# A hybrid DeltaNet and attention decoder in float32: the weights' low halves moved off GpSimd, intermediate results written into PSUM banks, and the output norm taken once per group of heads

## The chip, the cores and the metric

The kernel runs on one core of a Trainium2 chip. The metric is device time in microseconds (us) for one execution of the whole program. Engines are named as the profile names them: PE is TensorE (PEld its weight loads), DVE is VectorE, ACT is ScalarE, POOL is GpSimd and SP is SyncE, which here issues the DMAs. Each engine works through its own instructions in the order in which the program lists them, and an instruction starts when the semaphores that it waits for allow it.

## What is computed

A decoder trunk of two layers on 272 tokens (16 meta tokens and 256 of input) of width 2048, all in float32. Layer 0 mixes tokens by a gated DeltaNet, layer 1 by differential attention. Each has a squared-relu MLP of width 8192, and RMS norms stand around every part. Cut to what matters here, the DeltaNet is:

```python
proj = h @ w_in                                  # 2048 -> q, k, v, z, b, a
qkv  = silu(causal_depthwise_conv(qkv, conv_w))  # 4 taps
q, k = l2_normalize(q) * 128**-0.5, l2_normalize(k)
beta = sigmoid(b); g = -exp(a_log) * softplus(a + dt_bias)
o = chunk_gated_delta_rule(q, k, v, beta, g)     # a state S of 128 x 128 per head, by chunks
o = rms_norm(o, o_norm) * silu(z)                # the output norm, per head and token
mix = o @ w_out
h = h + rms_norm(mix, gain)
```

There are 16 query and key heads and 32 value heads of 128. The delta rule solves a unit triangular system per chunk and head, adds a correction to the state S, and reads S with the queries.

## The kernel before, in words

Activations lie with features on the 128 partitions and the 272 tokens along the row. Every float32 product is made of three fast ones (`mm3`, L147 to L159). A weight tile of 128x2048 arrives by DMA as `wraw`. `load_w` (L119 to L145) treats it in two halves of 1024 columns: ACT copies each to `whi`, a rounded type (L137), and another engine subtracts this from the raw half to give `wlo` (L141), here called the low half. PE then multiplies `whi` with `xh` (L154), `wlo` with `xh` (L157) and `whi` with `xl` (L158) for each of 16 blocks of 128. The second matmul of a half needs its low half. In the DeltaNet three `whi` and three `wlo` buffers rotate, each of half a tile; in the MLPs there are three more.

Which engine does L141 is decided at L138 to L140: while `ring["pool"]` is set, which is the whole DeltaNet, every second half of a tile goes to POOL and of the first halves every other one, and the rest goes to DVE. Outside the DeltaNet DVE does it, but for the first three tiles of three stages (two MLPs' and the query projection's), which POOL does while DVE is busy with a norm.

The DeltaNet (`gdn`) works on 8 groups of 4 value heads. PE's projections run without end: 12 tiles of `w_in` per group (4 for queries and keys, 4 for values, 4 for the gates z) and 4 tiles of `w_out` for the group two behind. The group's other work is written as Python generators in `Flow`, a list of tasks with due times. Each matmul of the projections advances a clock, and a task that is due places its instructions there; so the small matmuls of the delta rule stand among the projections, with the yields (`STEP`, `OTURN`, `SLACK` and so on) as distances. The build then sets the order within each engine. `tc.high_priority()` around a weight's halves puts them ahead.

The places that the prediction touches, in the order of a group:

- `conv_silu`, L606: four taps on a projection in PSUM (L615 on ACT, L618 on DVE), a tanh (L620, ACT, into the SBUF tile `cv_x`) and the product of both (L621, DVE, to `kq` or `vt`).
- `products`: norms of keys and queries, then for each chunk the products `ps_u`, multiplied by decays on DVE into `UA` (L711). POOL masks `UA` (L733, L826).
- `solve` with `forward`: 30 dependent small DVE instructions (L629, L630) on the 16x16 blocks.
- `core`: for each of three chunks of tokens (128, 128, 16) a chain of small matmuls through two PSUM banks (`bank`, tag "c") with an ACT or DVE instruction between each two. `w` is copied by ACT (L909), `ws` is `w` times a factor (L913, DVE), `ps_s2` the state's correction and `S` the new state (L925). `ps_o` is the output and `ov` its combination with the state's part (L936). Then the output norm: squares with sums on ACT (L942, into `o2`), eleven instructions of four columns on DVE (L944 to L948, with `rsqrt` at L105 to L111), and the scaling of `ov` by DVE (L949). `turned` transposes the result on PE (L809) and multiplies it by the gate (L811).
- `gate_out`: the product with `w_out`, added to `acc` by DVE (L982). For the last group each finished row block is also squared on ACT (`add_ss`, L183, or L185 on DVE for the last two) and summed into `ss` by DVE (L190), for the norm of the mix. `ss` goes to PE as `pst` (L213), and from there the first MLP begins.

Of the kernel before, what the change touches and what calls it, by code (L numbers as in the profile page):

```python
# [30 lines left out]
G1 = 8  # L31
GB = 4
HOLD = 1
QGAP = 3.0
# [1 line left out]
NSQ = 2  # L36
# [10 lines left out]
STEP7 = (2.0, 5.0, 35.0)  # L47
SLACK, UGAP, SOLVE, STEP, OTURN = 6.0, 1.2, 40.0, 3.0, 14.0
SQ = 2
PQ = 2  # L50
WARM = (2, 6, 8)
LAMBDA_INIT = 0.8 - 0.6 * math.exp(-0.3 * 1)
NEG = -1.0e30
# [34 lines left out]
def trunk(ctx: ExitStack, tc: tile.TileContext, a):  # L88
    nc = tc.nc
# [5 lines left out]
    npool = ctx.enter_context(tc.tile_pool(name="npool", bufs=2))  # L95
# [18 lines left out]
    ring = {"i": 0, "pools": [wpool] * 3, "spare": []}  # L114

    flow = Flow()
# [6 lines left out]
    def load_w(src, urgent=2, after=None):  # L123
        raw = load_raw(src)
        his, los = [], []
        with tc.high_priority() if urgent == 2 else ExitStack():
            for q in range(2):
                part = raw[:, q * HD:(q + 1) * HD]
                room = ring["spare"].pop(0) if ring["spare"] else None
                if room is None:  # L130
                    pool = ring["pools"][ring["i"] % len(ring["pools"])]
                    ring["i"] += 1
                    hi = pool.tile([P, HD], F32R, tag="whi", name="whi")
                    lo = pool.tile([P, HD], F32R, tag="wlo", name="wlo")
                else:
                    hi, lo = room
                nc.scalar.activation(hi, part, AF.Copy)  # L137
# [3 lines left out]
                inst = eng.tensor_tensor(lo, part, hi.bitcast(F32), ALU.subtract)  # L141
# [31 lines left out]
        pool, tag, bufs = ring["rows"]  # L173
        return pool.tile([P, L], F32, tag=tag, name=name, bufs=bufs)

    def add_ss(ss, src, m, N, eng):

        if m == 0:
            ss.append(npool.tile([P, L], F32, tag="ss", name="ss", bufs=1))
            return [nc.scalar.activation(ss[0][:, :N], src, AF.Square)]  # L180
        sq = npool.tile([P, L], F32, tag="sq", name="sq", bufs=SQ)
        if m < KT - NSQ or eng is nc.gpsimd:
            one = nc.scalar.activation(sq[:, :N], src, AF.Square)  # L183
# [6 lines left out]
        return [one, eng.tensor_tensor(ss[0][:, :N], ss[0][:, :N], sq[:, :N], ALU.add)]  # L190

    def squares(m, N, ss, acc, gi, after=None):

        inst = add_ss(ss, acc[:, m, :N], m, N, nc.vector)[-1].ins
# [87 lines left out]

    xh = xpool.tile([P, KT, L], F32R, tag="xh", name="xh")
    xl = xpool.tile([P, KT, L], F32R, tag="xl", name="xl")
    r0 = npool.tile([P, L], F32, name="r0", bufs=1)
    unscaled = {}
    with tc.tile_pool(name="ps0", bufs=2, space=bass.MemoryType.PSUM) as ps0:
        ring["p"] = v0
# [47 lines left out]
    ring["pool"] = True  # L336
# [4 lines left out]
    ring["pool"] = False  # L341


    qpool = ctx.enter_context(tc.tile_pool(name="qpool", bufs=1))
# [146 lines left out]
    ssm, e = mlp(0, L, xh, xl)  # L491
# [12 lines left out]
def gdn(ctx, tc, a, e):  # L504
    nc = tc.nc
    const, npool, dram, psm = (e[k] for k in ("const", "npool", "dram", "psm"))
# [3 lines left out]
    load_w, mm3, rsqrt, xh, xl, new_acc, ssm = (e[k] for k in ("load_w", "mm3", "rsqrt", "xh", "xl", "new_acc", "ssm"))  # L510
    squares, flow, r0 = e["squares"], e["flow"], e["r0"]
# [17 lines left out]
    def work(name):  # L529
        return gt.tile([P, HB, P], F32, tag="g1", name=name, bufs=G1)  # L530

# [75 lines left out]
    def conv_silu(ps, m, out):  # L607

        ac = gt.tile([P, L], F32, tag="g272", name="cv_a", bufs=GB)
        th = gt.tile([P, L], F32, tag="g272", name="cv_x", bufs=GB)  # L610
        x = ps
        if m in unscaled:
            x = th
# [6 lines left out]
        nc.scalar.activation(th, ac, AF.Tanh, scale=0.5)  # L620
        nc.vector.scalar_tensor_tensor(out, th, 1.0, ac, ALU.add, ALU.mult)  # L621

# [171 lines left out]
    def core(b, g):  # L794
# [7 lines left out]
        def turned(c, o, n, ov):  # L802

            while g["gates"] < HB:
                yield 1.0
            oT = g["oT"]
            pT = psc.tile([P, 512], F32, tag="c", name="ps_ot")
            for hv in range(HB):
                nc.tensor.transpose(pT[:, hv * n:(hv + 1) * n], ov[:n, hv], ident[:n, :n])  # L809
# [7 lines left out]
        step = STEP7[0] if b == NB - 1 else STEP  # L817
        merged = {}

        def flat(t):  # L820
# [38 lines left out]
        for c, (o, n) in enumerate(CH):  # L859
            if c == 0:  # L860
                R = nv[0]
            else:
# [12 lines left out]
                ov = work("ov")  # L875
# [29 lines left out]
                nc.tensor.matmul(pw[:n, hv], dt[:, hv, :], z[:n, hv], start=True, stop=True)  # L905
            if c == 2:
                g["free"] = True
            w = work("w")
            nc.scalar.copy(w[:n], pw[:n])  # L909
            if c < 2:  # L910
                ws = work("ws")
                sb = sup[:, c].rearrange("p h r -> p (h r)")[:, :, None].broadcast_to([P, HB, P])
                nc.vector.tensor_tensor(ws, w, sb, ALU.mult)  # L913
            yield step
            if c < 2:
                pS2, pS2v = bank("ps_s2")
# [19 lines left out]
                    nc.vector.scalar_tensor_tensor(ov[:n, hv], ov[:n, hv], eG[:n, c, HB * b + hv:HB * b + hv + 1],  # L936
                                                   po[:n, hv], ALU.mult, ALU.subtract)

            o2 = work("o2")
            ms = gt.tile([P, HB], F32, tag="o_ms", name="o_ms")  # L940
            for hv in range(HB):
                nc.scalar.activation(o2[:n, hv], ov[:n, hv], AF.Square, accum_out=ms[:n, hv:hv + 1])  # L942
            rqc = rq[:n, c].rearrange("p h r -> p (h r)")
            nc.vector.tensor_tensor(ms[:n], ms[:n], rqc, ALU.mult)  # L944
            nc.vector.tensor_tensor(ms[:n], ms[:n], rqc, ALU.mult)
            nc.vector.tensor_scalar(ms[:n], ms[:n], 1.0 / P, EPS, ALU.mult, ALU.add)
            ri = rsqrt(ms[:n], "rso", [P, HB], n)
            nc.vector.tensor_tensor(ri[:n], ri[:n], rqc, ALU.mult)  # L948
            nc.vector.tensor_tensor(ov[:n], ov[:n], ri[:n, :, None].broadcast_to([n, HB, P]), ALU.mult)  # L949
            g["chunk"] = c + 1  # L950
            flow.add(turned(c, o, n, ov), STEP7[1] if b == NB - 1 else OTURN)
            yield step

    def halves(g):
# [11 lines left out]
    def gate_out(b, g):  # L966

        if b == 0:
            flow.add(halves(g))
        flow.until(lambda: "halves" in g)  # L970
        oh, ol = g["halves"]
        for mq in range(4):
            hi, lo = load_w(a["w_out"][b, mq])
            for j in range(4):
                m = 4 * mq + j
                ps = psm.tile([P, 512], F32, tag="m", name="ps_out")
                mm3(ps[:, :L], hi, lo, 4 * j, oh, ol, HB, 0, L)
                with tc.high_priority():
                    if b == 0:
                        nc.scalar.copy(acc[:, m, :], ps[:, :L])  # L980
                    else:
                        added = nc.vector.tensor_tensor(acc[:, m, :], acc[:, m, :], ps[:, :L], ALU.add)  # L982
                    if b == NB - 1 and m > 0:
                        squares(m - 1, L, ssm, acc, 1, added)
                        if m == KT - 1:
                            squares(m, L, ssm, acc, 1)
        if b + 1 < NB:
            flow.add(halves(gs[b + 1]))

# [269 lines left out]
```

## Time and profile before

| what | value |
|---|---|
| median of 3 runs (lowest, highest) | 3111.37 us (3111.28, 3116.6) |
| the profiled execution, its own time | 3111.88 us |
| its span, first to last instruction | 3110.1 us |
| PE busy | 3010.9 us, 97% of the span |
| DVE busy | 1930.1 us, 62% |
| ACT busy | 1443.3 us, 46% |
| POOL busy | 660.7 us, 21% |
| mean granted TensorE clock | 0.987 of full |

The rows of the profile name a line, an engine, the operation, what is written and read (buffer numbers left out), the shape and the count. Then come the busy time, the mean of one in ns, and the idle time of that engine just before, with what ended it. A waits view sums such idle time by who waited for whom. A windows view gives for a stretch of time the busy time of each engine with its number of instructions, then the granted TensorE clock, the share of the DMA engines and GB/s. A timeline lists start, duration and instruction. A busy PE is not a PE at its peak, since matmuls overlap and their ends are modelled: the number of matmuls in a stretch says more than its busy time.

### The profile page before, as it was taken

The numbers are of one execution on the slowest core, as the hardware profiler recorded it, in microseconds if no ns is written. First come the engines' busy times: TensorE is split into PE (matmuls) and PEld (weight loads), VectorE is DVE, ScalarE is ACT, GpSimd is POOL, SyncE is SP. The second block draws the span as 40 slices with busy tenths as digits, with TensorE's granted clock in tenths as the row PEclk, the third lists the DMA queues.
The fourth block names the chain that finished last, engine by engine and source line by source line (L and its number), as shares of the span: only waits on it lengthen the run. The fifth ranks groups of instructions, "written<-read, shape, count | busy, mean of one in ns | idle before, by whom it ended". The sixth has DMA issues, their size and how long they took to land. (4 is left out here: it accounts for less than half of the span.)

```text
span 3110.1 us, 57337 instructions
## 1 busy us (share of the span) xinstructions
PE 3010.9 (97%) x23779; PEld 2946.4 (95%) x23779; DVE 1930.1 (62%) x3449; ACT 1443.3 (46%) x2565; POOL 660.7 (21%) x398
## 2 busy tenths in 40 slices
PE   7999999999998889999999999999999999999998
PEld 6988999999998889999999999999999999999998
DVE  7676574766748485455555557777756555555555
ACT  4445454454544345434444334555555444444443
POOL 2544445545454351000000003400004000000000
PEclk9999999999999989999999999999999999999999
DMA  4433334334343335454444443443354555555553
GB/s 178 151 117 122 133 118 151 133 125 158 117 152 103 119 145 183 176 176 172 171 174 175 176 176 123 177 149 136 138 189 163 189 186 183 188 189 180 188 190 109
DMA packets 92468, 488.36 MB, mean 157 GB/s; under 512 B 29104, under 2 KB 32528, under 8 KB 34736
## 3 DMA queue, kind: packets, MB, share of 16 engines
q1 hardware_dynamic: 92208, 484.70, 43.7%
q8 instruction: 187, 3.06, 0.4%
q14 instruction: 73, 0.60, 0.1%
HBM read 481.41 MB, written 3.25 MB: 156 GB/s over the span
## 5 line engine op out<-in xcount | busy, mean ns | idle before, releaser
L137 ACT ACTIVATE whi<-wraw 128x1024 fp32r<-128x1024 f32 x890 | 939.2, 1058 | 1180.3 <-PE ps_dn L158 435.9
L141 DVE TENSOR_TENSOR wlo<-wraw,whi 128x1024 fp32r<-128x1024 f32 x682 | 841.4, 1237 | 717.1 <-ACT whi L137 715.9
L141 POOL TENSOR_TENSOR wlo<-wraw,whi 128x1024 fp32r<-128x1024 f32 x208 | 503.7, 2424 | 1584.3 <-ACT whi L137 1572.5
L158 PE MATMUL ps_dn<-yl,whi 128*128 128x272 f32 (+1 forms) x2048 | 584.5, 285 | 0.0
L157 PE MATMUL ps_dn<-yh,wlo 128*128 128x272 f32 (+1 forms) x2048 | 583.2, 285 | 0.0
L154 PE MATMUL ps_dn<-yh,whi 128*128 128x272 f32 (+1 forms) x2048 | 583.2, 285 | 0.0
L154 PE MATMUL ps_up<-xh,whi 128*128 128x272 f32 (+1 forms) x2048 | 582.9, 285 | 0.0
L158 PE MATMUL ps_up<-xl,whi 128*128 128x272 f32 (+1 forms) x2048 | 582.0, 285 | 0.1
L157 PE MATMUL ps_up<-xh,wlo 128*128 128x272 f32 (+1 forms) x2048 | 581.5, 285 | 0.2 <-DVE wlo L141 0.2
L154 PE MATMUL ps_in<-xh,whi 128*128 128x272 f32 x1520 | 463.4, 305 | 0.0
L157 PE MATMUL ps_in<-xh,wlo 128*128 128x272 f32 x1520 | 442.4, 291 | 16.7 <-DVE wlo L141 13.3
L158 PE MATMUL ps_in<-xl,whi 128*128 128x272 f32 x1520 | 444.0, 292 | 3.3 <-DVE xl L319 3.3
L154 PEld LDWEIGHTS ps_up<-xh,whi 128*128 128x128 f32 x2048 | 386.2, 189 | 0.5 <-ACT xh L402 0.2
L158 PEld LDWEIGHTS ps_dn<-yl,whi 128*128 128x128 f32 x2048 | 386.6, 189 | 0.0
L154 PEld LDWEIGHTS ps_dn<-yh,whi 128*128 128x128 f32 x2048 | 386.3, 189 | 0.0
L158 PEld LDWEIGHTS ps_up<-xl,whi 128*128 128x128 f32 x2048 | 385.6, 189 | 0.3 <-DVE xl L410 0.3
L157 PEld LDWEIGHTS ps_dn<-yh,wlo 128*128 128x128 f32 x2048 | 385.2, 188 | 0.0
L157 PEld LDWEIGHTS ps_up<-xh,wlo 128*128 128x128 f32 x2048 | 384.7, 188 | 0.5 <-DVE wlo L141 0.5
L157 PEld LDWEIGHTS ps_in<-xh,wlo 128*128 128x128 f32 x1520 | 290.2, 191 | 20.3 <-DVE wlo L141 14.9
L154 PEld LDWEIGHTS ps_in<-xh,whi 128*128 128x128 f32 x1520 | 289.7, 191 | 7.8 <-issue 5.1
L158 PEld LDWEIGHTS ps_in<-xl,whi 128*128 128x128 f32 x1520 | 289.5, 190 | 4.8 <-DVE xl L319 3.7
L399 POOL TENSOR_TENSOR hT<-hT,t_res 128x272 f32<-128x272 f32 (+1 forms) x40 | 34.9, 894 | 742.9 <-DVE t_res L391 698.2
(305 smaller groups left out, 4833.8 us busy)
## 6 DMA issues: line engine op xcount, KB each, us to landing
wraw<-w_up SPq DMA_DIRECT2D x128, 1024.0 KB
wraw<-w_down SPq DMA_DIRECT2D x128, 1024.0 KB
wraw<-w_in SPq DMA_DIRECT2D x97, 1024.0 KB
wraw<-w_out SPq DMA_DIRECT2D x32, 1024.0 KB
wraw<-w_kv SPq DMA_DIRECT2D x32, 1024.0 KB
wraw<-w_q SPq DMA_DIRECT2D x16, 1024.0 KB
wraw<-w_o SPq DMA_DIRECT2D x16, 1024.0 KB
gb<-g_dram SPq DMA_DIRECT2D x8, 544.0 KB
```

The costliest lines, as they stand in the source:

```text
L137: nc.scalar.activation(hi, part, AF.Copy)
L141: inst = eng.tensor_tensor(lo, part, hi.bitcast(F32), ALU.subtract)
L154: one = nc.tensor.matmul(ps, wh, rh, start=(k == 0), stop=False)
L157: nc.tensor.matmul(ps, wl, rh, start=False, stop=False)
L158: ring["mm"] = nc.tensor.matmul(ps, wh, rl, start=False, stop=(k == nk - 1))
L399: put(key, eng.tensor_tensor(h, h, ts[m][:, :N], ALU.add))
```

## The change

All of it is in the DeltaNet, and in names and constants around it:

1. **Low halves.** The choice at L138 to L140 becomes `nc.gpsimd if not urgent else nc.vector`, and `ring["pool"]` goes. In the program POOL's L141 falls from 208 instructions to 18 (those first three tiles of three stages), and 190 move to DVE.
2. **Tanh through the bank.** `conv_silu` writes the tanh back into the projection's own PSUM bank, and L621 reads it there in place of `cv_x`.
3. **`ws` by ACT.** Four activations of 128x128 with a factor per partition read `ps_w` and write `ws`; only then comes the copy to `w`. The DVE instruction of 128x512 (L913) goes.
4. **The output norm per group.** The squares are written into the PSUM bank of `ps_o` in place of `o2`. In groups 0 to 6 the eleven small DVE instructions run once for the three chunks (12 columns) in place of three times (4 columns). Each chunk's `ov` is scaled by four activations on ACT in place of L949. The three transposes then follow at `OTURN`, `OTURN + 2` and `OTURN + 4`. In the last group the norm stays per chunk, with ACT's four activations.
5. **Squares of the mix through banks.** In the last group's `gate_out` a square is written by ACT into the PSUM bank of the row block that has just been added to `acc`, and `ss` adds it from there. The squares of the last two row blocks move from DVE to ACT too.
6. **Room.** `G1`, the number of 128x512 work tiles, goes from 8 to 9, and `r0` shares the buffer of `ss`.

```diff
-                ring["n"] = ring.get("n", 0) + 1
-                on_pool = ring.get("pool") and (q == 1 or ring["n"] // 2 % PQ == 1)
-                eng = nc.gpsimd if not urgent or on_pool else nc.vector
+                eng = nc.gpsimd if not urgent else nc.vector
...
-    def add_ss(ss, src, m, N, eng):
+    def add_ss(ss, src, m, N, eng, bank=None):
...
-        sq = npool.tile([P, L], F32, tag="sq", name="sq", bufs=SQ)
-        if m < KT - NSQ or eng is nc.gpsimd:
+        if bank is None or m == KT - 1:
+            sq = npool.tile([P, L], F32, tag="sq", name="sq", bufs=SQ)
+        else:
+            sq = bank
+        if m < KT - NSQ or eng is nc.gpsimd or bank is not None:
             one = nc.scalar.activation(sq[:, :N], src, AF.Square)
...
-        th = gt.tile([P, L], F32, tag="g272", name="cv_x", bufs=GB)
...
+        th = ps[:, :L]
         nc.scalar.activation(th, ac, AF.Tanh, scale=0.5)
         nc.vector.scalar_tensor_tensor(out, th, 1.0, ac, ALU.add, ALU.mult)
...
+            if c < 2:
+                ws = work("ws")
+                for hv in range(HB):
+                    nc.scalar.activation(ws[:, hv], pw[:, hv], AF.Copy, scale=sup[:, c, hv // 2, hv % 2:hv % 2 + 1])
             w = work("w")
             nc.scalar.copy(w[:n], pw[:n])
-            if c < 2:
-                ws = work("ws")
-                sb = sup[:, c].rearrange("p h r -> p (h r)")[:, :, None].broadcast_to([P, HB, P])
-                nc.vector.tensor_tensor(ws, w, sb, ALU.mult)
...
-            o2 = work("o2")
-            ms = gt.tile([P, HB], F32, tag="o_ms", name="o_ms")
             for hv in range(HB):
-                nc.scalar.activation(o2[:n, hv], ov[:n, hv], AF.Square, accum_out=ms[:n, hv:hv + 1])
...
-            nc.vector.tensor_tensor(ov[:n], ov[:n], ri[:n, :, None].broadcast_to([n, HB, P]), ALU.mult)
+                nc.scalar.activation(po[:n, hv], ov[:n, hv], AF.Square, accum_out=ms[:n, c, hv:hv + 1])
+            outs.append((c, o, n, ov))
+            if b == NB - 1 or c == len(CH) - 1:
...
+                ri = rsqrt(mc, "rso%d" % k, [P, k], pn)
+                nc.vector.tensor_tensor(ri, ri, rqc, ALU.mult)
+                for i, (cc, oo, nn, ot) in enumerate(outs):
+                    for hv in range(HB):
+                        nc.scalar.activation(ot[:nn, hv], ot[:nn, hv], AF.Copy, scale=ri[:nn, HB * i + hv:HB * i + hv + 1])
+                    flow.add(turned(cc, oo, nn, ot), STEP7[1] if b == NB - 1 else OTURN + TGAP * i)
```

Lines after the first edit move by up to ten: L139 of the changed kernel is L141 of the one before, L191 is L190, L616 is L618, L620 is L621, L710 is L711, L927 is L925, L938 is L936 and L991 is L982.

On DVE, in a group of the middle, where the second chunk's state `S` and output `ov` are formed, the kernel before has, with `oT` the gated output and `o_ms` the sums of squares:

```order
L811 SCALAR_TENSOR_TENSOR oT<-ps_ot,gain_h,oT 128x4x128
L621 SCALAR_TENSOR_TENSOR vt<-cv_x,cv_a 128x272
L711 SCALAR_TENSOR_TENSOR UA_4838<-ps_u,sc_nc,dec 16x32
L913 TENSOR_TENSOR ws<-w,sc_sup 128x512
L925 SCALAR_TENSOR_TENSOR S<-S,eGL,ps_s_4910 128x128 x4
L936 SCALAR_TENSOR_TENSOR ov<-ov,eG,ps_o 128x128 x4
L618 SCALAR_TENSOR_TENSOR cv_a<-ps_in,gdnc,cv_a 128x271
L618 SCALAR_TENSOR_TENSOR cv_a<-ps_in,gdnc,cv_a 128x270
L944 TENSOR_TENSOR o_ms<-o_ms,sc_rq 128x4
```

At the same place of the changed kernel's DVE there stands:

```order
L139 TENSOR_TENSOR wlo<-wraw,whi 128x1024
L620 SCALAR_TENSOR_TENSOR vt<-ps_in,cv_a 128x272
L710 SCALAR_TENSOR_TENSOR UA_4763<-ps_u,sc_nc,dec 16x32 x2
L927 SCALAR_TENSOR_TENSOR S<-S,eGL,ps_s_4832 128x128
L139 TENSOR_TENSOR wlo<-wraw,whi 128x1024
L927 SCALAR_TENSOR_TENSOR S<-S,eGL,ps_s_4832 128x128 x3
L938 SCALAR_TENSOR_TENSOR ov<-ov,eG,ps_o 128x128 x4
L616 SCALAR_TENSOR_TENSOR cv_a<-ps_in,gdnc,cv_a 128x271
```

`ws` and the norm's small instructions are gone from here, `vt` reads the tanh from the bank `ps_in`, and two low halves stand in the queue, one of them between the first and the other three parts of `S`.

On ACT, near a group's end, where the third chunk's squares are taken and the gates' tanh (`zt`) follow, the kernel before has:

```order
L942 ACTIVATE o_8289,o_ms<-ov 16x128 x4
L137 ACTIVATE whi<-wraw 128x1024
L790 ACTIVATE zt<-ps_in 128x272
L772 ACTIVATE nv<-ps_v,sc_nk 128x128 x2
L772 ACTIVATE nv<-ps_v,sc_nk 16x128
L137 ACTIVATE whi<-wraw 128x1024 x2
L790 ACTIVATE zt<-ps_in 128x272
```

There the changed kernel's ACT has, with the scaling of the three chunks' `ov` at L957:

```order
L137 ACTIVATE whi<-wraw 128x1024 x2
L789 ACTIVATE zt<-ps_in 128x272
L137 ACTIVATE whi<-wraw 128x1024
L957 ACTIVATE ov<-ov,rs_y 128x128 x8
L137 ACTIVATE whi<-wraw 128x1024
L957 ACTIVATE ov<-ov,rs_y 16x128 x4
L789 ACTIVATE zt<-ps_in 128x272
```

Eight activations that wait for DVE's `rs_y` now stand between two upper halves of weights, and four more behind.

More of the change, by code (lines that the diff above doesn't have):

```diff
@@ L30 @@
 LAG = 2
-G1 = 8
+G1 = 9
 GB = 4
@@ L49 @@
 SQ = 2
-PQ = 2
+TGAP = 2.0
 WARM = (2, 6, 8)
@@ L190, in add_ss, with squares @@
         return [one, eng.tensor_tensor(ss[0][:, :N], ss[0][:, :N], sq[:, :N], ALU.add)]
-    def squares(m, N, ss, acc, gi, after=None):
-        inst = add_ss(ss, acc[:, m, :N], m, N, nc.vector)[-1].ins
+    def squares(m, N, ss, acc, gi, after=None, bank=None):
+        inst = add_ss(ss, acc[:, m, :N], m, N, nc.vector, bank)[-1].ins
         if m < PRE[gi // 2]:
@@ L284, in trunk @@
     xl = xpool.tile([P, KT, L], F32R, tag="xl", name="xl")
-    r0 = npool.tile([P, L], F32, name="r0", bufs=1)
+    r0 = npool.tile([P, L], F32, tag="ss", name="r0", bufs=1)
     unscaled = {}
@@ L334, in trunk @@
     nc.vector.tensor_scalar(nlam, nlam, -1.0, None, ALU.mult)
-    ring["pool"] = True
     ssm = []
@@ L609, in conv_silu @@
         ac = gt.tile([P, L], F32, tag="g272", name="cv_a", bufs=GB)
-        th = gt.tile([P, L], F32, tag="g272", name="cv_x", bufs=GB)
         x = ps
         if m in unscaled:
-            x = th
+            x = gt.tile([P, L], F32, tag="g272", name="cv_x", bufs=GB)
             nc.vector.tensor_tensor(x, ps[:, :L], r0, ALU.mult)
@@ L817, in core @@
         step = STEP7[0] if b == NB - 1 else STEP
+        outs = []
+        ms = gt.tile([P, len(CH), HB], F32, tag="o_ms", name="o_ms")
+        nc.vector.memset(ms, 1.0)
         merged = {}
@@ L983, in gate_out @@
                     if b == NB - 1 and m > 0:
-                        squares(m - 1, L, ssm, acc, 1, added)
+                        squares(m - 1, L, ssm, acc, 1, added, spent)
                         if m == KT - 1:
-                            squares(m, L, ssm, acc, 1)
+                            squares(m, L, ssm, acc, 1, None, ps)
+                spent = ps
         if b + 1 < NB:
```

17 lines of the change are left out of this document (9 added, 8 removed).

## The prediction

> **What bounds the kernel now.** The first view read is the table of windows: PE's, PEld's, DVE's, ACT's and POOL's busy time with its count of instructions, then the granted clock, the DMA share and GB/s. Its rows are the DeltaNet without its start and end, the end of the DeltaNet, and a stretch of the MLP.
>
> ```profile
> 60.00:1088.00 1028.00, 973.24 (x7459) 932.45 (x7457) 663.61 (x1499) 490.67 (x1118) 491.95 (x258) 0.98 0.37 130
> 1088.00:1137.00 49.00, 37.21 (x247) 36.20 (x248) 36.09 (x50) 18.17 (x31) 26.30 (x12) 0.80 0.49 176
> 1400.00:1800.00 400.00, 400.00 (x3174) 400.00 (x3173) 216.59 (x265) 164.93 (x202) 0.00 (x0) 1.00 0.49 174
> ```
>
> In the MLP PE never stops: 3174 matmuls in 400 us, 0.126 us each, at full clock. Nothing there can be shortened by this change. In the DeltaNet's body PE stands still for 1028 − 973.2 = 54.8 us, and its clock averages 0.98, worth at most 0.02 × 1028, about 20 us. At the end another 11.8 us of 49 are idle. So about 85 us can be had at all, between 30 and 1137 us. The DMAs are busy 0.37 of the time and aren't the limit.
>
> Second comes the waits view of PE for 30 to 1135 us: who waited for whom, us in all, times, the longest.
>
> ```profile
> PE ps_in L157 <- DVE wlo L141: 12.8, 6, 5.2
> PE pst L213 <- DVE ss L190: 10.6, 1, 10.6
> PE ps_s L918 <- DVE ws L913: 9.8, 7, 3.4
> PE ps_ot L809 <- DVE ov L949: 8.1, 3, 4.5
> PE ps_u L705 <- DVE UA L711: 6.8, 5, 1.4
> PE ps_out L154 <- DVE acc L982: 4.8, 5, 2.5
> PE ps_g L579 <- issue: 3.5, 1, 3.5
> PE ps_in L157 <- POOL wlo L141: 3.4, 4, 1.6
> ```
>
> Nearly every row names DVE, which is busy only 663.6 of 1028 us, 65%. So the question is why a DVE with time to spare comes late. Third, then, are the timelines (start, duration, instruction) of DVE and of POOL around one such wait:
>
> ```profile
> 553.89 2.27 DVE L109 SCALAR_TENSOR_TENSOR rs_t<-rs_t 128x12 f32<-128x12 f32 x1
> ...
> 565.48 2.40 DVE L621 SCALAR_TENSOR_TENSOR vt<-cv_x,cv_a 128x272 f32<-128x272 f32 x1
> ```
>
> ```profile
> 553.77 2.36 POOL L141 TENSOR_TENSOR wlo<-wraw,whi 128x1024 fp32r<-128x1024 f32 x1 [2.37 <-ACT whi L137]
> 565.19 2.38 POOL L141 TENSOR_TENSOR wlo<-wraw,whi 128x1024 fp32r<-128x1024 f32 x1 [9.06 <-ACT whi L137]
> ```
>
> A DVE instruction on 12 columns takes 2.27 us and ends at 556.16; POOL's low half, which began just before it, ends at 556.13. The product `vt` ends at 567.88, POOL's next at 567.57. An instruction that meets POOL's low half stands until that is over. What decides which instructions do this shows in DVE's groups (busy us, mean ns | idle before) and in the tile view of `acc` (min/median/max ns):
>
> ```profile
> L141 DVE TENSOR_TENSOR wlo<-wraw,whi 128x1024 fp32r<-128x1024 f32 x63 | 79.4, 1261 | 122.4 <-ACT whi L137 121.8
> ...
> L621 DVE SCALAR_TENSOR_TENSOR kq<-cv_x,cv_a 128x272 f32<-128x272 f32 x32 | 35.6, 1113 | 20.5 <-ACT cv_x L620 20.5
> ...
> L621 DVE SCALAR_TENSOR_TENSOR vt<-cv_x,cv_a 128x272 f32<-128x272 f32 x32 | 34.4, 1075 | 7.9 <-ACT cv_x L620 7.6 <-PE ps_v L770 0.3
> L949 DVE TENSOR_TENSOR ov<-ov,rs_y 128x512 f32<-128x512 f32 (+1 forms) x24 | 24.6, 1025 | 0.3
> L190 DVE TENSOR_TENSOR ss<-ss,sq 128x272 f32<-128x272 f32 x14 | 20.8, 1485 | 0.3 <-ACT sq L183 0.2
> ```
>
> ```profile
> L982 DVE TENSOR_TENSOR acc<-acc,ps_out x112: 399/436/442, 483.4 to 1126.3; 128x272 f32<-128x272 f32 x112
> ```
>
> `ss` and `acc` add the same 128x272. With both inputs in SBUF the mean is 1485 ns; with one in PSUM not one of 112 took over 442 ns. The change removes the collision from both sides: POOL's low halves go, and three of the DVE operations get an input in PSUM.
>
> **What it costs and saves, part by part.** The profiled execution took 3111.88 us, 1.78 more than its span and 0.5 more than the median of 3111.37; the sum is made against it.
>
> *Low halves.* 190 go to DVE at 1.261 us, 240 us. Against that stand 24.6 us of L949, and the products and sums at 0.436 instead of their means: 70.0 − 64 × 0.436 = 42 and 20.8 − 14 × 0.436 = 15. DVE's load rises by at most 240 − 25 − 42 − 15 = 158 us, to (664 + 158)/1028 = 80%; the small instructions that no longer stand, as the one at 553.89, take part of it back. DVE doesn't become the bound by its sum. Its queue is the risk: it works in order, and the order puts two low halves among the instructions of `S` and `ov`, so 2 × 1.26 us fall into a chain on which the next chunk's products wait. Their cover are the matmuls of the projections between two steps. I take 1 us for each of 8 groups, **+8 us** (0 to 2 × 1.26 × 8 = 20).
>
> *Waits that end.* The waits on `wlo` of both engines, `ws`, `ov`, `UA` and `acc` sum to 12.8 + 3.4 + 9.8 + 8.1 + 6.8 + 4.8 = 45.7 us. One of them stands in the end of the DeltaNet, on the last group's path, and isn't counted:
>
> ```profile
> 1087.25 0.58 PE L809 MATMUL ps_ot<-ident,ov 16*128 16x16 f32 x4 [4.55 <-DVE ov L949]
> ```
>
> That leaves 41. Not each is the collision's alone: behind the late DVE instruction the chain would sometimes be late by itself. I take two thirds, **−28 us** (0 to −46).
>
> *The clock.* Two of the longest waits were followed by stretches of 7 us with the clock near 0.6:
>
> ```profile
> 208.00:215.00 7.00, 7.00 (x33) 6.64 (x34) 6.83 (x16) 1.50 (x7) 2.34 (x1) 0.61 0.39 139
> 341.00:348.00 7.00, 6.90 (x35) 6.61 (x36) 1.73 (x5) 0.81 (x1) 2.77 (x3) 0.60 0.27 38
> ```
>
> Each costs 0.4 × 7 = 2.7 us. With the third at the end such waits cost about 8; two thirds as above, **−5 us** (0 to −20, the body's whole clock loss). [...]
>
> *The end.* PE's last product of the DeltaNet and the first of the MLP after it, and the same boundary behind the first MLP, which has no POOL work in DVE's way that PE's matmuls don't cover:
>
> ```profile
> 1116.19 0.29 PE L158 MATMUL ps_out<-ol,whi 128*128 128x272 f32 x1
> ...
> 1136.59 0.37 PE L154 MATMUL ps_up<-xh,whi 128*128 128x272 f32 x1
> ```
>
> ```profile
> 1913.38 0.29 PE L158 MATMUL ps_dn<-yl,whi 128*128 128x272 f32 x1
> ...
> 1924.93 0.36 PE L154 MATMUL ps_at<-yh,whi 128*128 128x256 f32 x1
> ```
>
> These are 20.4 and 11.6 us. DVE now lags behind PE because each `ss` add collides (14 × 1.49 us). With squares in PSUM a row block needs 2 × 0.436 us of DVE, and its 48 matmuls last 48 × 0.126 = 6 us per weight tile, in which DVE also has two low halves, 2.5 us. It keeps up, so the second distance replaces the first: **−9 us** (0 to −9). What is late next is the norm itself.
>
> *ACT.* `ws` (16 × 4 activations) and the scaling of `ov` (24 × 4) come to ACT:
>
> ```profile
> L137 ACT ACTIVATE whi<-wraw 128x1024 fp32r<-128x1024 f32 x257 | 270.9, 1057 | 293.7 <-PE ps_in L158 174.3 <-PE ps_out L158 79.1 <-issue 16.0
> ...
> L942 ACT ACTIVATE o<-ov 128x128 f32<-128x128 f32 (+1 forms) x96 | 28.7, 301 | 39.0 <-DVE ov L936 37.9
> L772 ACT ACTIVATE nv<-ps_v,sc_nk 128x128 f32<-128x128 f32 (+1 forms) x96 | 27.9, 351 | 13.6 <-PE ps_v L770 13.4
> ```
>
> No row has them; the nearest are activations of this shape from SBUF (0.301) and with a factor from PSUM (0.351). 160 × 0.301 to 0.351 is 48 to 56 us, ACT at most (491 + 56)/1028 = 53%. What counts is the burst of 12 scalings once per group, which waits for DVE's norm with the next `whi` behind it in ACT's queue: 12 × 0.351 = 4.2 us. A half of a weight feeds 24 matmuls, 3.0 us; with three buffers a freed one is wanted again after 6.0, and 1.06 + 1.26 are needed to fill it, which leaves 3.7. So a burst shows 0.5 us, 8 groups **+4 us** (0 to 8 × 4.2 = 34, if nothing covers it). `ws` stands where the copy and the product stood, 4 × 0.351 against 0.58 and more; nothing.
>
> *Banks.* The bank of a projection is held longer by tanh and product, under 1 us; four rotate, each filled for 6 us, so nothing (were that cover gone, 64 × 0.9 us). The bank of `ps_o` is now held until the squares are written, and the next chunk's products need its pair:
>
> ```profile
> 541.88 0.19 ACT L942 ACTIVATION_READ_ACCUMULATOR o<-ov 128x1 f32 x1
> ```
>
> ```profile
> 543.75 1.03 PE L870 MATMUL ps_qs<-S,kq 128*128 128x256 f32 x4
> ```
>
> The last square ends at 542.07 and `ps_qs` begins 1.7 us later; the matmuls between cover it, at nothing (without them, 16 waits of up to that size). More room and the shared `r0` cost nothing.
>
> Sum: 8 − 28 − 5 − 9 + 4 = −30, and 3111.9 − 30 = **3082 us**.
>
> **The rivals.** *Slower: low halves late on DVE.* The stretch has 127 weight tiles (254 halves, of which POOL now does three in four), and PE needs a low half after its second matmul. If DVE's queue delays each tile beyond the 3.7 us of slack so that PE waits a mean 0.5 us, that is 63 us against the 42 of all gains: +21, **3133 us**. It decides from 42/127 = 0.33 us a tile. For it speaks that the largest wait is already on DVE's own `wlo` and that DVE's own count of halves becomes four times as large; against it that those waits come with POOL's collisions and that DVE is idle a fifth of the time at least. Chance 0.14.
>
> *The port, the other way.* POOL keeps its masks of `UA`, and a DVE low half can hold POOL up as POOL held DVE. [...] As a mechanism of this kernel: a mask that waits 1.26 us delays the solve or `ps_o`, and the waits in the body stay with another name, as they also do if the chains are late by themselves. Then only the end gains: −9 + 4 = −5, **3107 us**. Against it: POOL's low halves, 2.36 us each, stood in POOL's own queue ahead of the masks, and go. Chance 0.13.
>
> *All of it.* Every wait of the list and the clock's 8 us go and nothing new comes: −46 − 8 − 9 = −63, with the +4 of ACT **3053 us**. Against it: chains rarely lose all their waits. Chance 0.13.
>
> **How the numbers follow.** The forecast has 0.60; its own range is 3066 to 3099: all 41 us of waits and 8 of the clock with new costs of 12 give 3066, half of both with new costs of 20 give 3099. The range that holds the time 8 in 10 runs from the best case at 3053 to past the third at 3112; it leaves out the slower rival and some tail. About 0.2%, 6.2 us, is what a measurement of this kernel can tell from no change. Faster by more: 0.60 + 0.13 and a little of the third, 0.75. Within: most of the third, 0.11. Slower: the first rival, 0.14.
>
> **What would show it.** In the changed profile: DVE's 272-column `kq`, `vt` and `ss` at a mean near 0.44 us; POOL's L141 18 times; the first MLP's first matmul 30 us sooner, near 1107 us; the boundary at about 11.5 us; `ps_s` no longer waiting for `ws`. I am wrong if PE's waits for `wlo` grow past 20 us, if waits for ACT (`whi`, `ov`) appear beyond 10, or if the boundary stays at 20.

## The result and the profile after

The changed kernel takes 3034.1 us (median of 4 runs, 3032.05 to 3036.74) against 3111.55 us before: a ratio of 0.975, 95% interval 0.9735 to 0.9765, so 77 us less. The prediction had the direction and the mechanism, but at 3082 us, with a range from 3053 to 3112, far too little of it. The profiled execution took 3035.05 us, its span is 3033.3 us; against the 3111.88 us of before that is 76.8 us.

To see where they came from, both programs are cut at the same instructions: the first matmul of the second group's projections, the first product with `w_out` after the last projection, the last such product, the first product of the MLP. So each stretch holds the same work. The windows of before (columns as in the prediction) are:

```profile
0.00:123.55 123.55, 100.39 (x648) 92.64 (x649) 92.37 (x170) 54.80 (x114) 48.12 (x38) 0.93 0.44 163
123.55:1034.55 911.00, 872.60 (x6739) 838.68 (x6737) 586.23 (x1318) 442.67 (x1012) 445.37 (x232) 0.99 0.38 132
1034.55:1116.19 81.64, 73.15 (x541) 68.69 (x540) 51.31 (x115) 33.90 (x69) 30.99 (x15) 0.92 0.37 131
1116.19:1136.59 20.40, 9.82 (x56) 9.22 (x54) 14.20 (x23) 4.22 (x6) 10.34 (x5) 0.67 0.43 159
```

And those of the changed kernel, cut at the same matmuls (the last row runs 0.05 us past the MLP's first product, which starts at 1064.95):

```profile
0.00:102.31 102.31, 93.16 (x647) 86.71 (x648) 75.79 (x164) 53.69 (x114) 6.89 (x18) 1.00 0.55 200
102.31:972.02 869.71, 866.90 (x6738) 834.26 (x6737) 627.18 (x1324) 482.50 (x1152) 57.38 (x72) 1.00 0.40 138
972.02:1055.40 83.38, 74.30 (x542) 68.64 (x540) 52.10 (x126) 42.52 (x93) 8.63 (x4) 0.90 0.36 128
1055.40:1065.00 9.60, 8.19 (x56) 7.50 (x54) 5.53 (x13) 2.39 (x5) 5.96 (x4) 0.82 0.80 308
```

| stretch | before us | after us | difference |
|---|---|---|---|
| start and first group | 123.55 | 102.31 | −21.2 |
| the other groups | 911.00 | 869.71 | −41.3 |
| last group's end | 81.64 | 83.38 | +1.7 |
| DeltaNet to MLP | 20.40 | 9.55 | −10.9 |
| all behind it | 1973.5 | 1968.4 | −5.1 |

In the first two stretches PE's idle time (length less busy time) falls from 23.2 + 38.4 = 61.6 to 9.2 + 2.8 = 12.0 us, by 49.6. The rest of their 62.5, 12.9 us, is PE's busy time for the same matmuls. I put it down to the clock, which goes from 0.93 and 0.99 to 1.00 in both. In 870 us of the body PE now stands still for 2.8.

PE's waits in the changed kernel, with the longest few from the start to the end of the DeltaNet (engine, tile and line, for whom; us in all, times, the longest):

```profile
PE ps_in L305 <- DVE xg L297: 8.3, 1, 8.3
PE ps_ot L808 <- ACT ov L957: 6.9, 3, 5.5
PE ps_kn L647 <- DVE kq L620: 2.0, 1, 2.0
PE ps_qs L872 <- ACT ps_o L942: 1.8, 1, 1.8
```

The first is the start of the program, as before. The rows for `wlo`, `ws`, `UA` and `acc` have no successor over 0.3 us: no matmul waits for a low half any more, though DVE makes nearly all of them. DVE's groups of 30 to 1064 us (busy us, mean ns):

```profile
L139 DVE TENSOR_TENSOR wlo<-wraw,whi 128x1024 fp32r<-128x1024 f32 x252 | 310.5, 1232 | 186.8 <-ACT whi L137 186.2
...
L628 DVE TENSOR_TENSOR fw_t<-xt,na 68x32 f32<-68x32 f32 (+14 forms) x120 | 52.4, 436 | 2.2
...
L620 DVE SCALAR_TENSOR_TENSOR vt<-ps_in,cv_a 128x272 f32<-128x272 f32 x32 | 13.9, 435 | 6.0 <-ACT ps_in L619 3.5 <-PE ps_v L769 2.5
...
L191 DVE TENSOR_TENSOR ss<-ss,ps_out 128x272 f32<-128x272 f32 x14 | 6.0, 430 | 0.1
```

`vt` falls from 1075 to 435 ns and the sums `ss` from 1485 to 430, as forecast. The small instructions of the triangular solve, `fw_t`, which no edit touched, fell too; before they took

```profile
L629 DVE TENSOR_TENSOR fw_t<-xt,na 68x32 f32<-68x32 f32 (+14 forms) x120 | 74.6, 621 | 2.0
```

621 ns each, now 436. With the low halves of POOL added, DVE's busy time in the second stretch rises only from 586 to 627 us, 72% of it; the prediction had allowed for 80%.

### The profile page after: what moved, and what is told of

Read it like the earlier page. It is cut to its first block, busy times and chain, and to the rows that moved or that the text cites. A ratio compares the mean times of both kernels' runs of the same rounds, so it can differ in the third digit from the quotient of the medians.

```text
span 3033.3 us, 57216 instructions
## 1 busy us (share of the span) xinstructions
PE 2992.3 (99%) x23779; PEld 2928.8 (97%) x23779; DVE 1946.6 (64%) x3451; ACT 1489.2 (49%) x2727; POOL 205.8 (7%) x208
## 5 line engine op out<-in xcount | busy, mean ns | idle before, releaser
L139 DVE TENSOR_TENSOR wlo<-wraw,whi 128x1024 fp32r<-128x1024 f32 x872 | 1071.1, 1231 | 777.7 <-ACT whi L137 777.0
L475 DVE TENSOR_TENSOR acc<-acc,ps_dn 128x272 f32<-128x272 f32 (+1 forms) x224 | 96.1, 429 | 122.0 <-PE ps_dn L156 121.3
L152 PE MATMUL ps_at<-xh,whi 128*128 128x272 f32 x512 | 154.4, 302 | 0.0
```

The lines of the kernel that those rows point to most:

```text
L152: one = nc.tensor.matmul(ps, wh, rh, start=(k == 0), stop=False)
L475: nc.vector.tensor_tensor(acc[:, m, :N], acc[:, m, :N], ps[:, :N], ALU.add)
```

## The experiments

The theory, called the theory of the port in the expectations (a name only: no run shows what the two engines share): POOL's low half, a subtraction of two SBUF tiles that takes 2.4 us, stops every DVE instruction that needs both inputs from SBUF, and PE's waits and the clock losses behind them are the price. The rivals: POOL's result itself comes late (2.4 us in place of 1.2); or the other edits carry the gain by shortening chains; or DVE's queue only has room for the low halves because of those edits. Times are medians of four or five runs, and ratios stand against the kernel before on the same chip (3111.8 to 3113.4 us there, 3111.55 beside the changed kernel), so a difference of 1 or 2 us between two experiments can be the chip's. The code cuts leave out the counter behind `on_pool`, the flag that limits it to the DeltaNet, the allocation of the unused tile `junk`, and for the three edits the lines of `add_ss` that stand under the change.

**Only the low halves moved.**

```diff
 # the kernel before
-                eng = nc.gpsimd if not urgent or on_pool else nc.vector
+                eng = nc.gpsimd if not urgent else nc.vector
```

> The kernel before with the first edit alone: 190 low halves move from POOL to DVE, all else as before. Theory of the port (POOL's low half stops every DVE instruction that has both inputs in SBUF until it ends): without POOL's halves there is nothing to collide with, so most of the 77 us come, 3035 to 3055 us; the 272-column products kq and vt fall from 1.1 us to about 0.44 without any help of PSUM. Theory of the edits (tanh and squares in banks, the norm once per group and ACT's scalings shorten the chains): 3085 to 3105 us. Theory of the queue (DVE's load of low halves needs the other edits to make room for it): slower than 3111 us, with PE's waits for wlo over 20 us.

Measured: 3045.4 us, ratio 0.9786 (0.9771 to 0.9800), 67 of the 77 us. `kq` and `vt` take 452 and 451 ns with the tanh still in SBUF:

```profile
L619 DVE SCALAR_TENSOR_TENSOR kq<-cv_x,cv_a 128x272 f32<-128x272 f32 x32 | 14.5, 452 | 3.3 <-ACT cv_x L618 3.3
L619 DVE SCALAR_TENSOR_TENSOR vt<-cv_x,cv_a 128x272 f32<-128x272 f32 x32 | 14.4, 451 | 3.8 <-ACT cv_x L618 2.9 <-PE ps_v L768 0.9
```

"Both inputs from SBUF" is too narrow for the victims, though. `L105`, an instruction of the norm with one SBUF input, shows the same fall on its smallest form, first in the kernel before and then here:

```profile
L105 DVE TENSOR_SCALAR rs_y<-o_ms 16x4 int32<-16x4 int32 x8 | 12.0, 1497 | 0.1
```

```profile
L105 DVE TENSOR_SCALAR rs_y<-o_ms 16x4 int32<-16x4 int32 x8 | 1.2, 151 | 0.0
```

Cut as above, the DeltaNet up to the last projection ends 64.2 us sooner than before, against 62.5 in the changed kernel. So in the body this edit is the whole gain, and the edits of tanh, `ws` and the norm add nothing to it. What is left of PE's waits:

```profile
PE pst L211 <- DVE ss L188: 9.9, 1, 9.9
PE ps_in L302 <- DVE xg L294: 8.1, 1, 8.1
PE ps_ot L807 <- DVE ov L947: 6.6, 3, 4.5
```

The wait for the sum of squares `ss` at the end stays.

**All but the low halves.** The changed kernel with the old choice of engine.

```diff
 # the changed kernel
-                eng = nc.gpsimd if not urgent else nc.vector
+                eng = nc.gpsimd if not urgent or on_pool else nc.vector
```

> The changed kernel with the low halves divided between POOL and DVE as before. Theory of the port: what still has both inputs in SBUF collides again; kq, vt and ss don't, since they read a bank. 3070 to 3095 us. Theory of the edits: 3035 to 3055 us.

Measured: 3100.2 us, ratio 0.9962 (0.9949 to 0.9975): 12.5 us less than before, 5 us short of what the port's theory gave at least, and none of it from the body, which ends 2.4 us later than before. Its second stretch, in before's window, and two groups of DVE:

```profile
123.55:1034.55 911.00, 874.93 (x6741) 837.35 (x6741) 503.35 (x1137) 479.89 (x1151) 431.11 (x232) 0.99 0.38 133
```

```profile
L633 DVE TENSOR_TENSOR fw_t<-xt,na 68x32 f32<-68x32 f32 (+14 forms) x120 | 96.8, 807 | 3.0
...
L625 DVE SCALAR_TENSOR_TENSOR vt<-ps_in,cv_a 128x272 f32<-128x272 f32 x32 | 14.0, 438 | 25.7 <-ACT ps_in L624 23.8 <-PE ps_v L774 1.9
```

DVE is busy for 503 us there in place of 586, and PE stands still as long as ever (36 us; 38 before). `vt` no longer collides, but what comes behind it does: `fw_t` goes from 621 to 807 ns. Here, taking single victims out of the way (`vt` from 1075 to 438 ns) handed the collision to others in the queue.

**POOL reads, for nothing.** DVE makes the low halves; POOL does the same subtraction into a tile that nobody reads, at the old places.

```diff
 # the changed kernel, the old condition as on_pool
                 inst = eng.tensor_tensor(lo, part, hi.bitcast(F32), ALU.subtract)
+                if on_pool:
+                    nc.gpsimd.tensor_tensor(junk, part, hi.bitcast(F32), ALU.subtract)
```

> The changed kernel, in which POOL, at the 190 places where it made a low half before, does the same subtraction once more into a tile that nobody reads (of a narrower type); DVE makes the low half that is used. Theory of the port: the collisions are back though no result of POOL's is waited for: 3065 to 3095 us, about as with the halves back on POOL. Theory of the late result (a low half from POOL takes 2.4 us in place of 1.2 and comes late): 3030 to 3040 us, no change.

Measured: 3159.2 us, ratio 1.0152 (1.0137 to 1.0167), 125 us over the changed kernel, and nothing reads the result of these subtractions. That rules out the late result. The loss is larger than expected. Part of the reason shows: the low halves on DVE have two SBUF inputs too and become victims. Their mean rises from 1232 to 1614 ns, and now PE does wait for them.

```profile
L140 DVE TENSOR_TENSOR wlo<-wraw,whi 128x1024 fp32r<-128x1024 f32 x248 | 400.2, 1614 | 133.1 <-ACT whi L138 132.8
```

```profile
PE ps_in L159 <- DVE wlo L140: 28.5, 20, 2.5
```

**POOL writes, for nothing.** In place of that subtraction a copy of one column (so that it starts when `whi` is there) and two fills of the unused tile.

```diff
+                if on_pool:
+                    nc.gpsimd.tensor_copy(junk[:, :1], hi.bitcast(F32)[:, :1])
+                    nc.gpsimd.memset(junk, 0)
+                    nc.gpsimd.memset(junk, 0)
```

> The same as the kernel with POOL's idle subtraction, but at those places POOL copies one column and then fills the unused tile twice, which reads nothing: about 2 us of writing. Theory of the port, in the form that only POOL's reads stop DVE: 3032 to 3042 us, no change. In the form that any POOL instruction stops it: 3060 to 3095 us.

Measured: 3038.3 us, ratio 0.9762 (0.9746 to 0.9778), against 0.975 for the changed kernel. That is 4 us more, with overlapping intervals, where POOL's reading cost 125. POOL is nearly as busy as with the idle subtraction (546.7 us from 30 to 1140 us in the copies and fills, 565.0 there in the subtractions), so its own masks stand behind as much work (977 ns in the mean for `UA`, 912 there), and ACT waits 46.5 us in all for POOL to give back a `whi` buffer, against 20.4 us there. DVE's low halves keep a mean of 1236 ns and `fw_t` 451, where with the subtraction they had 1614 and 856. So it isn't POOL's being busy, nor its writing, nor its late release of buffers, nor a delay of its masks, but its reading. The tile view of the unused tile (min/median/max ns):

```profile
L145 POOL MEMSET junk<- x189: 949/951/956, 29.5 to 1052.1; 128x1024 int8 x189
L143 POOL CAST junk<-whi x188: 186/1172/1723, 34.2 to 1049.9; 128x1 int8<-128x1 f32 x188
```

The fills hardly vary (949 to 956 ns). The copy of one column takes 186 ns at best and 1172 in the median, near the 1236 of DVE's low half. One starts at 561.24 us, behind a low half that started at 560.98; the low half ends at 562.21 and the copy at 562.26. So the collision goes both ways: here POOL's copy stands until DVE's low half is over, as DVE's `vt` in the kernel before ended at 567.88 us, behind POOL's low half at 567.57.

**The squares of the mix through SBUF again.**

```diff
 # the changed kernel
-                        squares(m - 1, L, ssm, acc, 1, added, spent)
+                        squares(m - 1, L, ssm, acc, 1, added)
-                            squares(m, L, ssm, acc, 1, None, ps)
+                            squares(m, L, ssm, acc, 1)
```

> The changed kernel with the fifth edit undone: the squares of the mix go through SBUF again. With the first edit alone PE still waited 9.9 us at the end of the DeltaNet for the sum of squares. Theory of the port: the six low halves of the MLP's first tiles that stay on POOL still stop the sums that read SBUF, so that wait is back, 3041 to 3046 us. Theory that the end was long for other reasons (ACT's scaling in the last group, the norm itself): 3033 to 3037 us, no change.

Measured: 3042.5 us, ratio 0.9772 (0.9759 to 0.9786), 8 us over the changed kernel (7 by the ratios), and the wait for `ss` is back. The waits view and the tile view of `ss` (min/median/max ns):

```profile
PE pst L214 <- DVE ss L191: 9.9, 1, 9.9
```

```profile
L191 DVE TENSOR_TENSOR ss<-ss,sq x14: 427/434/2530, 1037.7 to 1063.9; 128x272 f32<-128x272 f32 x14
```

Six low halves of the MLP's first weights stay on POOL in both kernels, just there. The bank takes the sums out of their way (430 ns in the mean in the changed kernel, 2530 for the longest here).

**Three edits alone.** Low halves on DVE, squares of the mix through banks, `r0` in the buffer of `ss`; nothing else.

```diff
 # the kernel before
-                eng = nc.gpsimd if not urgent or on_pool else nc.vector
+                eng = nc.gpsimd if not urgent else nc.vector
-                        squares(m - 1, L, ssm, acc, 1, added)
+                        squares(m - 1, L, ssm, acc, 1, added, spent)
-                            squares(m, L, ssm, acc, 1)
+                            squares(m, L, ssm, acc, 1, None, ps)
-    r0 = npool.tile([P, L], F32, name="r0", bufs=1)
+    r0 = npool.tile([P, L], F32, tag="ss", name="r0", bufs=1)
```

> The kernel before with three edits alone: the low halves on DVE, the squares of the mix through banks, and r0 in the buffer of ss. The tanh, ws, the norm and the number of work tiles stay as before. Theory that the collisions were all with POOL's low halves, so that the edits of tanh, ws and norm save nothing once these are gone: 3028 to 3032 us, a little under the changed kernel, since the last group's scaling stays on DVE. Theory that those edits carry a part: 3036 us and more.

Measured: 3029.9 us, ratio 0.9732 (0.9719 to 0.9745), the fastest of these kernels, about 4 us under the changed kernel (6 by the ratios).

**`r0` alone, beside the low halves.**

```diff
 # the kernel with only the low halves moved
-    r0 = npool.tile([P, L], F32, name="r0", bufs=1)
+    r0 = npool.tile([P, L], F32, tag="ss", name="r0", bufs=1)
```

> The low halves on DVE and r0 in the buffer of ss, all else as before: beside the kernel with the first edit alone this only moves what is allocated behind r0 by the 1088 bytes a partition that it no longer takes. The changed kernel runs the second MLP in 730.6 us where the kernel before and the one with the first edit alone take 736.5, with the clock full and no waits. Theory that the place of the tiles in SBUF sets the pace of the matmuls there: the second MLP in 730.6 us, the whole in 3038 to 3041 us. Theory that another edit or chance does it: 3044 to 3047 us.

Measured: 3038.7 us, ratio 0.9762 (0.9748 to 0.9775), 6.7 us under the kernel without it. 200 us of its second MLP, and the same window of the kernel with the low halves alone:

```profile
2530.00:2730.00 200.00, 200.00 (x1706) 200.00 (x1705) 114.86 (x142) 89.16 (x111) 0.00 (x0) 1.00 0.52 187
```

```profile
2530.00:2730.00 200.00, 200.00 (x1693) 200.00 (x1692) 113.96 (x141) 88.02 (x109) 0.00 (x0) 1.00 0.52 186
```

PE never stops in either, the clock is full, and 0.8% more matmuls are done, from the last product of the attention's output to the end 730.6 to 731.1 us in place of 736.5.

**The last group's end: scaling on DVE.** The changed kernel takes 1.7 us longer than before in its third stretch, where the kernel with the low halves alone takes 2.5 less.

```diff
 # the changed kernel
+                    if b == NB - 1:
+                        nc.vector.tensor_tensor(ot[:nn], ot[:nn], ri[:nn, :, None].broadcast_to([nn, HB, P]), ALU.mult)
-                    for hv in range(HB):
+                    for hv in range(HB if b < NB - 1 else 0):
```

> The changed kernel with the last group's output scaled by one DVE instruction a chunk, as before, in place of four activations on ACT; the other groups stay on ACT. In the changed kernel the stretch from the last product of the projections to the last of w_out takes about 4 us longer than with the first edit alone. Theory that ACT's scaling, in a queue with the halves of the weights, costs this: 3028 to 3031 us. Theory that the longer wait only stands in for another (the squares, the gate): 3033 to 3037 us.

Measured: 3035.1 us, ratio 0.9748 (0.9735 to 0.9762): no change, and the theory that ACT's scaling costs the time falls. The wait is 5.8 us, now for DVE. In the trace the third stretch is 1.8 us shorter than the changed kernel's, but PE's idle time there is not (9.5 us against 9.1); the clock is 0.92 against 0.90:

```profile
972.86:1054.42 81.56, 72.04 (x541) 68.31 (x540) 54.25 (x129) 38.99 (x81) 8.63 (x4) 0.92 0.37 131
```

**The last group's end: squares in SBUF.**

```diff
 # the changed kernel
-                nc.scalar.activation(po[:n, hv], ov[:n, hv], AF.Square, accum_out=ms[:n, c, hv:hv + 1])
+                sq2 = work("o2") if b == NB - 1 else po
+                nc.scalar.activation(sq2[:n, hv], ov[:n, hv], AF.Square, accum_out=ms[:n, c, hv:hv + 1])
```

> The changed kernel, but in the last group alone the squares of the output norm go to a tile in SBUF, as before, in place of the bank of ps_o; the scaling stays on ACT. In the changed kernel the last group's stretch is 4 to 5 us longer than with the first edit alone, and moving the scaling back to DVE didn't shorten it. Theory that the bank is at fault (PE waits 1.8 us for it, and a square into a bank starts 0.43 us after the one before, in place of 0.30): 3029 to 3032 us. Theory that it is the scaling and the order together, not the bank: 3033 to 3037 us.

Measured: 3031.3 us, ratio 0.9740 (0.9726 to 0.9755); the profiled span is 2.5 us under the changed kernel's. The intervals overlap, but in the trace the place is plain: the wait of `ps_qs` for the bank is gone and the longest for `ov` falls from 5.5 to 4.3. In the changed kernel's ACT timeline the squares of the last chunk start 0.43 us apart:

```profile
1022.91 0.27 ACT L942 ACTIVATE ps_o<-ov 16x128 f32<-16x128 f32 x1 [4.38 <-DVE ov L938]
1023.12 0.18 ACT L942 ACTIVATION_READ_ACCUMULATOR ps_o<-ov 16x1 f32 x1
1023.34 0.27 ACT L942 ACTIVATE ps_o<-ov 16x128 f32<-16x128 f32 x1
```

and in before's, into SBUF, 0.30:

```profile
1083.19 0.31 ACT L942 ACTIVATE o<-ov 16x128 f32<-16x128 f32 x1 [4.38 <-DVE ov L936]
1083.40 0.19 ACT L942 ACTIVATION_READ_ACCUMULATOR o<-ov 16x1 f32 x1
1083.50 0.29 ACT L942 ACTIVATE o<-ov 16x128 f32<-16x128 f32 x1
```

The third stretch of this kernel:

```profile
970.93:1052.16 81.23, 73.99 (x541) 68.64 (x540) 52.15 (x126) 41.73 (x93) 8.63 (x4) 0.92 0.36 131
```

It takes 81.2 us, against 83.4 in the changed kernel and 79.0 with three edits alone. PE's idle time is 7.2 us, against 9.1 and 7.7, so the bank accounts for that part, 1.8 us. The rest of the 4.4 us goes with the granted clock (0.92, 0.90 and 0.94), and why that differs isn't settled; bank and scaling undone together weren't tried.

**More low halves on DVE.** How much room had its queue? About 64 and about 127 of the low halves are done a second time, into an unused tile (the condition is for 64; with its first half alone it is 127).

```diff
 # the changed kernel
                 inst = eng.tensor_tensor(lo, part, hi.bitcast(F32), ALU.subtract)
+                if q == 1 and ring["n"] // 2 % PQ == 1:
+                    nc.vector.tensor_tensor(junk, part, hi.bitcast(F32), ALU.subtract)
```

> The changed kernel, in which DVE does about 64 of the low halves a second time, into a tile that nobody reads, directly behind the one that is used: DVE's queue of the DeltaNet grows by 64 x 1.23 = 79 us, its busy share there from 71% to about 79%. Theory that the queue has room to spare (no matmul waits for a low half in the changed kernel): 3033 to 3038 us, no change. Theory of the queue (each delay of a low half soon shows): a third of the added time or more, 3055 us and up.

> The same with the second half of every weight tile done twice, about 127 more: 156 us, DVE's busy share about 87%. Theory of room to spare: the room ends here, a few matmuls wait for low halves and for the small chains, 3040 to 3065 us. Theory of the queue: half of the added time or more, 3100 us and up.

Measured: 3048.3 us, ratio 0.9796 (0.9779 to 0.9812), and 3060.5 us, ratio 0.9833 (0.9818 to 0.9847): 14 us for 78 us of added work on DVE and 26 for 157 (the busy time of the second subtractions). Each added microsecond costs about 0.17 to 0.18, so neither "no change" nor "a third" holds for the first; the second lies in the range of room to spare. Windows of 150 to 900 us, of the changed kernel, and with 64 and 127 more:

```profile
150.00:900.00 750.00, 749.60 (x5837) 721.48 (x5836) 536.68 (x1142) 422.60 (x1017) 48.22 (x60) 1.00 0.40 138
```

```profile
150.00:900.00 750.00, 746.24 (x5794) 716.25 (x5794) 579.89 (x1154) 418.98 (x1006) 46.74 (x60) 1.00 0.39 136
```

```profile
150.00:900.00 750.00, 744.83 (x5754) 712.28 (x5753) 622.66 (x1199) 413.86 (x992) 44.42 (x60) 1.00 0.39 137
```

At 623/750 = 83% PE still loses only 83 of 5837 matmuls, 10 us. In both traces the waits for `wlo` are 1.8 us in all, and the cost is spread over the start, small chains and the last group. Nothing like a DVE that becomes the bound.

## Why the prediction was wrong in size

*What bounds the kernel* held. PE's idle time and clock in the DeltaNet were the 85 us that could be had, the collision with POOL's reads (125 us for idle reads, 4 for writes) was what kept them, and the four experiments on it leave none of the rivals as the cause of the bulk. The signs that the prediction named came: `kq` and `vt` at 435 ns and `ss` at 430, 18 low halves on POOL, no wait of `ps_s` for `ws`. Only the MLP's first matmul came 71.6 us sooner, where 30 was forecast.

*Waits that end, −28.* This is the first step that failed. The collision's share was taken as two thirds of 41 us of listed waits. The windows show PE's idle time of the first two stretches falling by 49.6 us: not two thirds of the listed, but nearly all there was. Two things were wrong. The discount supposed that chains would be late by themselves; with no collision hardly any was (2.8 us of idle time are left in the body, 2.0 of them the wait for `kq`, which stayed). And the sum was over rows with DVE's name that seemed to belong to the change, while others that were left out ended too: `vt` (3.0 us), most of `xl` (3.3 to 0.8) and the 3.5 us put down to issue. The whole idle time of the windows was the better bound. The 4.55 us of the last group's `ps_ot`, which the prediction did leave out, stayed (5.48).

*The clock, −5.* Measured 12.9. The prediction gave the body's loss as at most 20 and then counted only three long waits; the start, in a slower clock (0.93 over the first 124 us), was not in its windows.

*Low halves on DVE, +8.* Measured: nothing; no matmul waits for one. The order of DVE's queue, with two low halves among the parts of `S`, was read rightly, but PE has other work for such a delay: 157 us more of them cost 26. The rival built on this, 3133 us, is out, and so is the one by which the masks on POOL would be held up instead: their mean goes from 916 to 989 ns, and no wait of PE's over 0.3 us is for `UA`.

*ACT, +4, and the banks.* In the body nothing. In the last group the bank did cost: `ps_qs` waits 1.8 us for the squares. The cover that the prediction named, matmuls of the projections, is gone there, and its price per wait was right; it didn't ask where the cover ends.

*The end, −9.* Measured −10.9, by the way forecast (`ss` 430 ns in the mean, the boundary at 9.55 us); undoing the edit costs 7 to 8 us.

*Room, at nothing.* Measured −5 to −7, by the place of `r0`. The prediction's sentence that nothing in the MLP can be shortened took a PE that never stops for one at its best pace; no row of the profile before showed otherwise.

So −49.6 − 12.9 + 1.7 − 10.9 − 5.1 = −76.8, where 8 − 28 − 5 − 9 + 4 stood. The rival "all of it", 3053 us, was the nearest, and fell short mainly by the clock, by the rows left out and by `r0`.

## What to carry to other kernels

Where POOL reads SBUF for long stretches, look at the spread of DVE's durations by group. Here a DVE instruction on 12 columns that took 2.27 us beside POOL's 2.36, and a group with a PSUM operand that stayed at 399 to 442 ns (`acc`), showed that POOL's time was taken out of DVE's, and moving that work onto a DVE that was two thirds busy gained 67 us. Take away the instruction that the others stand behind, not its victims one by one: that one edit gave 67 of the 77 us, the others without it 12.5. When one cause stands behind all of a stage's waits, price its removal by the stage's idle time and clock loss together, and discount only for a chain that can be named.

## What the runs showed of the hardware beyond that

- Moving tiles by 1088 bytes a partition, with the same instructions, changed the pace of a stage in which PE never waits from 1693 to 1706 matmuls in 200 us. What in the place of the tiles does it isn't shown.
- A square of 16x128 into a PSUM bank with its sum read after it started 0.43 us after the one before, into SBUF 0.30, though the activation itself was shorter (0.27 against 0.29 to 0.31 us).
- The clock halved behind a wait of 2.0 us. The changed kernel's PE is busy up to 119.5 us, stands still until 121.46, and then, in windows of 1 us:

```profile
121.00:122.00 1.00, 0.54 (x5) 0.53 (x6) 0.96 (x4) 0.00 (x0) 0.00 (x0) 1.00 0.96 401
122.00:123.00 1.00, 1.00 (x10) 1.00 (x9) 0.84 (x2) 0.96 (x3) 0.00 (x0) 0.94 0.52 201
123.00:124.00 1.00, 1.00 (x7) 1.00 (x6) 0.61 (x1) 1.00 (x6) 0.42 (x3) 0.50 0.00 0
124.00:125.00 1.00, 1.00 (x6) 1.00 (x6) 0.96 (x2) 0.17 (x2) 1.00 (x2) 0.50 0.14 16
125.00:126.00 1.00, 1.00 (x7) 1.00 (x6) 0.00 (x0) 0.00 (x0) 0.92 (x2) 0.50 0.13 19
126.00:127.00 1.00, 1.00 (x9) 1.00 (x8) 0.00 (x0) 0.30 (x1) 0.00 (x0) 0.85 0.16 18
```

The clock falls about 1.4 us after PE is back at work and stays at half for about 3.4 us, an estimate from the 0.94 and the 0.85 of these windows. In the kernel before, PE waits 2.06 us up to 47.72 us and 1.92 us up to 241.51 us, and the clock stays full behind both:

```profile
47.00:54.00 7.00, 6.28 (x50) 5.98 (x51) 6.27 (x18) 5.58 (x23) 3.79 (x2) 1.00 0.43 152
241.00:248.00 7.00, 6.49 (x52) 6.47 (x53) 3.81 (x9) 3.67 (x7) 3.28 (x3) 1.00 0.41 150
```

So the length of the wait alone, 1.96 us with the fall and 2.06 without, doesn't decide it; what else does isn't shown.
